# Compressed-branch scores as eight small tiles of the array, compressed values split in two, and chunk products in pairs, in a one-core transformer layer

## The chip, the core and the metric

The kernel runs on one core of a Trainium2 chip. The metric is the device time of one execution in microseconds (us). A core has a matrix engine (TensorE, PE in the profile, with its weight loads as PEld), a vector engine (VectorE, DVE), an activation engine (ScalarE, ACT), a general engine (GpSimd, POOL) and a queue that issues transfers (SyncE, SP). Each works through its own list of instructions in order and waits on semaphores for the others. PE reads SBUF and writes PSUM, which holds eight banks of 128 partitions by 512 float32 values here.

## What is computed

One decoder layer on 512 positions and 1024 features. One input projection feeds two token mixers; mixer A is sparse attention with a compressed, a selected and a window branch, mixer B a gated linear recurrence in chunks of 64. Both are gated, projected, summed, projected again and normalized.

```python
h = x @ w_in + b_in                          # 5912 columns, split into ten parts
kc, vc = compress(k_cmp, ...), compress(v_cmp, ...)       # 31 blocks per group
sc = einsum('bghqd,bgnd->bghqn', q, kc) * scale           # 8 heads, 2 groups
o_cmp = masked_softmax(sc, cmp_end <= t) @ vc
o_a = g0 * o_cmp + g1 * o_slc + g2 * o_win
attn = where(causal, einsum('bhncd,bhnsd->bhncs', qe, ke), 0)   # chunks of 64
o_b = attn @ v + carried state
y = sigmoid(gm_a) * (o_a @ w_branch_a) + sigmoid(gm_b) * (o_b @ w_branch_b)
x = layer_norm(alpha * x + y @ w_out)
```

With 512 positions the selected branch takes all eight blocks, so that both it and the window are plain causal attention.

## The kernel before

**Number formats.** Large products are made in three passes: each operand is split by `split2` (ACT copies it to float32r, DVE subtracts to get the rest), and hi·hi, hi·lo, lo·hi are summed in PSUM. A float32r product is one record in the trace. A product of plain float32 operands is two records.

**Stages.** The gate tiles of mixer B come first, then `proj(name)` makes one 128-column tile of the input projection after another in the order of `SEQ`: kcmp, vcmp, kslc, kwin, q0, q1, v, zb0, q2, zb1, q3, zb2, zb3, za0 to za3, then the sixteen gate tiles. A tile is 24 products of 512 columns. Then come the branch projections in the order of `BRANCH` (each entry two outputs of 12 products, written to a `pa` and a `pss` bank), and the output projection over four row blocks.

**What sets the order.** PE and SP keep the program's order. All smaller work is in generators ("chains") run by `_Weave`: every second step of a projection calls `tick()`, which lets each chain that is due go on to its next `yield`; the number yielded is the ticks to wait. The table `D` holds these numbers. ACT and DVE have their order fixed by the scheduler when the program is built.

**Mixer B.** `hgrn(h)` makes for each of four heads the chunk products `pst_`: four of 64 weight columns and 64 moving columns (first chunk of each pair with itself), four of 128 weight columns and 64 moving columns. `hgrn_norm` then sends the norms to all partitions with sixteen small SP transfers in a row and waits `n2` ticks.

**The compressed branch.** `cmp_kv` makes the compressed keys and values with three small float32 products in three `pst` tiles (two buffers); keys go to `kcB` in a block-diagonal form of 64 columns. `cmp_probs(c)`, for c = 0 and 1, multiplies each 128-row block of two query tiles `qraw` (weights) by `kcB` (64 moving columns): four products per query tile, 16 in all, in float32; the result has positions on partitions, so the softmax follows directly. It ends with `transpose4` into `PTc[c]`. `attn_values` begins with four float32 products of `vcB` and `PTc`, 512 columns each.

**Loads.** `load(i + 3)` puts the weights of a later tile into one of three `wraw` buffers, `split(i + 2)` splits them. Query tiles also issue four small SP transfers each (`rope`). The query tile's own copy out of PSUM is the ACT instruction at line 332 (in `evac`).

**The end.** In each branch step the kernel loads a block of the output weights (`load_out`), subtracts row means (`minus_mean`) and splits it. The output projection uses the banks `pa` and `pss` in turn, and at the last block also `pst`.

Of the kernel before, what the change touches and what calls it, by code (L numbers as in the profile page):

```python
# [43 lines left out]
BRANCH = [("b", 0), ("b", 2), ("a", 0), ("b", 4), ("a", 2), ("b", 6), ("a", 4), ("a", 6)]  # L44


def _columns(name):

    c = np.arange(_COLS[name], _COLS[name] + 128)
    if name[0] == "q" and name[1] != "b" or name[:2] == "za":  # L50
# [17 lines left out]
         r0=5, p0=5, p1=13, a0=1, a1=3, a2=1, a3=1, a4=1, a5=1, s0=14, s1=21, s2=0, s3=2)  # L68
# [27 lines left out]
def layer_kernel(ctx: ExitStack, tc: tile.TileContext, xT, xn, w0, wi, wf, wv, small, brow, consts,  # L96
# [141 lines left out]
    kcB = cst.tile([P, 64], F32, name="kcB")  # L238
# [4 lines left out]
    G.memset(kcB, 0.0)  # L243
# [121 lines left out]
    def hgrn(h):  # L365
# [44 lines left out]
        V.copy_predicated(at[0:64].rearrange("p (t s) -> p t s", s=128),  # L410
                          tri[0:64].unsqueeze(1).to_broadcast([64, 4, 128]),
                          pst_[0:64].rearrange("p (t s) -> p t s", s=128))
        V.copy_predicated(chunks(at[64:128])[:, :, 1],
                          tri[64:128, 64:128].unsqueeze(1).to_broadcast([64, 4, 64]),
                          chunks(pst_[64:128])[:, :, 1])
# [27 lines left out]
    def hgrn_norm():  # L443
# [19 lines left out]
        yield D["n2"]  # L463
# [31 lines left out]
    mvs, ready = [None, None], set()  # L495

    def cmp_kv():
# [24 lines left out]
        T.matmul(ps[:, 0:64], w2s[:, 0:128], hT[:, 0:64], start=True, stop=True)  # L522
        for g in range(2):
            V.tensor_copy(kcB[64 * g:64 * g + 64, 32 * g:32 * g + 32], ps[64 * g:64 * g + 64, 32 * g:32 * g + 32])
        for g in range(2):
            ps = PT()
            T.matmul(ps[:, 0:64], hT[:, 64 + 128 * g:192 + 128 * g], w2s[:, 128:192], start=True, stop=True)
            for m in range(4):
                r = 32 * (2 * (m % 2) + g)
                dst = vcB[r:r + 32, m, 64 * g:64 * g + 64]  # L530
                if m % 2:
                    V.tensor_copy(dst, ps[r:r + 32, 0:64])
                else:
                    A.copy(dst, ps[r:r + 32, 0:64])
        ready.add("cmp")

# [51 lines left out]
    def cmp_probs(c):  # L588
        while "cmp" not in ready:
            yield 1  # L590
        ps = PS()
        for m in range(2):
            for i in range(4):
                T.matmul(ps[:, 128 * i + 64 * m:128 * i + 64 * m + 64],
                         qraw[2 * c + m][:, 128 * i:128 * i + 128], kcB, start=True, stop=True)
            if m == 0:
                yield 1
        s = T2()
        s4 = s.rearrange("p (i h n) -> p i h n", i=4, n=32)
        s3 = s.rearrange("p (x n) -> p x n", n=32)  # L600
        mx = SM(16, "mx")
        V.tensor_tensor(s4, ps.rearrange("p (i h n) -> p i h n", i=4, n=32),
                        cmask.unsqueeze(2).to_broadcast([P, 4, 4, 32]), ALU.add)
# [14 lines left out]
        PTc[c] = T2()  # L618
        A.copy(PTc[c], ps)
# [47 lines left out]
    def attn_values():  # L667

        while len(PTc) < 2:
            yield 1  # L670
        for m in range(4):
# [110 lines left out]
    for name in SEQ:  # L782
# [8 lines left out]
        if name[0] == "q":  # L791
# [52 lines left out]

    y, rb = [], {}
    load_out(0)
    for n, (mix, m0) in enumerate(BRANCH):
# [3 lines left out]
        load_out(n + 1)  # L851
# [22 lines left out]
        hl = [(T2(dt=F32R), T2(dt=F32R)) for _ in range(2)]  # L874
        nm = minus_mean(woraw[n])
        for raw, (hi, lo) in zip(woraw[n], hl):
            A.activation(hi, raw, AF.Identity, bias=nm)
# [131 lines left out]
```

## Time and profile before

| | |
|---|---|
| time, median of 3 runs | 441.57 us (440.76 to 441.75) |
| the profiled execution | 441.97 us, of which the span is 440.2 us |
| PE busy | 431.6 us, 98% of the span |
| DVE busy, ACT busy, POOL busy | 299.4, 244.8 and 16.6 us |
| granted TensorE clock | 0.997 of full speed |
| chain that ended last | PE 89%, DVE 3%, SP queue 2%, ACT 2% |

The span runs from the first to the last instruction; about 1.8 us of the execution lie around it. A row of the timeline gives start, duration, engine, line, operation, output<-input tiles, shape and how many records (x) are merged. Matmuls overlap their successors, so that a product's price is the distance from its start to that of the next, and not its duration. "[0.77 <-ACT t L332]" says that the engine sat idle for 0.77 us and what ended the wait.

### The profile page before, as it was taken

What the parts mean: (1) busy time and instruction counts of PE and PEld (TensorE: products, weight loads), DVE (VectorE), ACT (ScalarE), POOL (GpSimd) and SP (SyncE); (2) the same over time, 40 slices, a digit from 0 to 9 for tenths busy, and PEclk for the clock granted to TensorE, in tenths of its full rate; (3) what the DMA queues carried; (4) which work ended last, traced back from release to release, by engine and by line L of the source; (5) the groups of instructions that cost most, each with busy time, mean ns of one, the idle gap of its engine ahead of it and who ended that gap; (6) DMA issues with size and microseconds to landing.
All of it is one profiled execution on the core that took longest, in us unless ns stands there. A gap on an engine that the chain in (4) does not pass through costs nothing.

```text
span 440.2 us, 6100 instructions
## 1 busy us (share of the span) xinstructions
PE 431.6 (98%) x2205; PEld 361.2 (82%) x2205; DVE 299.4 (68%) x619; ACT 244.8 (56%) x488; POOL 16.6 (4%) x28
## 2 busy tenths in 40 slices
PE   9999999999999999999999999999999999999994
PEld 8888888888898887887888888888888888878884
DVE  5815769986887339965664667666755598882675
ACT  4444625413447326679765676678955577657300
POOL 2000000000011310000000010001001100000000
PEclk9999999999999999999999999999999999999998
DMA  7996300342320363221211112111223452153121
GB/s 270 394 349 212 133 0 2 96 145 76 107 85 0 87 224 117 100 96 49 95 48 49 48 50 96 49 48 48 95 72 123 127 210 94 48 171 117 50 95 48
DMA packets 20878, 47.57 MB, mean 108 GB/s; under 512 B 2928, under 2 KB 4592, under 8 KB 20848
## 3 DMA queue, kind: packets, MB, share of 16 engines
q1 hardware_dynamic: 20560, 46.92, 31.4%
q8 instruction: 17, 0.28, 0.3%
q10 hardware_dynamic: 288, 0.26, 0.2%
q14 instruction: 13, 0.11, 0.1%
HBM read 41.93 MB, written 2.10 MB: 100 GB/s over the span
## 4 chain that ended last, share of the span: by engine, by line
PE 89%; DVE 3%; SPq 2%; ACT 2%; DMA 1%; issue 1%; POOL 0%; DVEq 0%; ACTq 0%
PE pa L104 56%; PE pss L104 19%; PE pso L104 10%; PE pst L108 4%; SPq L111 2%; DMA wraw<-in_wf_dram 1%; PE pst L104 1%; ACT whi L147 1%; DVE wlo L148 0%; ACT t L147 0%; DVE t L148 0%; DVE t L878 0%; DVE t L866 0%; POOL gat L317 0%; DVE t L926 0%
## 5 line engine op out<-in xcount | busy, mean ns | idle before, releaser
L104 PE MATMUL pa<-t,whi 128*128 128x512 f32 x640 | 203.4, 399 | 0.3 <-ACT t L811 0.3
L104 PEld LDWEIGHTS pa<-t,whi 128*128 128x128 f32 x640 | 116.8, 188 | 25.8 <-issue 2.3
L104 PE MATMUL pa<-t,wlo 128*128 128x512 f32 x320 | 125.2, 391 | 0.0
L148 DVE TENSOR_TENSOR wlo<-wraw,whi 128x1024 fp32r<-128x1024 f32 x46 | 56.7, 1234 | 29.8 <-ACT whi L147 29.8
L104 PEld LDWEIGHTS pa<-t,wlo 128*128 128x128 f32 x320 | 60.0, 188 | 13.2
L147 ACT CAST whi<-wraw 128x1024 fp32r<-128x1024 f32 x46 | 48.2, 1047 | 34.0 <-PE pa L104 16.0
L104 PE MATMUL pss<-t,t 128*128 128x512 f32 (+5 forms) x302 | 48.2, 315 | 0.0
L104 PE MATMUL pa<-t,t 128*128 128x512 f32 (+1 forms) x216 | 48.0, 379 | 0.1
L104 PEld LDWEIGHTS pa<-t,t 128*128 128x128 f32 x216 | 39.3, 188 | 7.9 <-DVE t L866 0.5
L104 PEld LDWEIGHTS pss<-t,t 128*128 128x128 f32 (+1 forms) x302 | 38.7, 173 | 6.5 <-issue 1.0
L651 ACT ACTIVATE t<-t,sm_mn 128x512 f32<-128x512 f32 (+3 forms) x64 | 35.8, 560 | 14.8 <-DVE sm_mn L648 13.7
L648 DVE CUSTOM_DVE_ANT_0 t<-pss,t 128x512 f32<-128x512 f32 (+3 forms) x64 | 30.1, 487 | 16.9 <-PE pss L104 16.8
L148 DVE TENSOR_TENSOR t<-pst,t 128x512 fp32r<-128x512 f32 x40 | 27.5, 689 | 15.8 <-ACT t L147 15.8
L147 ACT CAST t<-pst 128x512 fp32r<-128x512 f32 x40 | 23.1, 579 | 17.1 <-PE pst L108 16.9
L108 PE MATMUL pst<-con,t 128*128 128x128 f32 x181 | 27.4, 272 | 0.0
L108 PEld LDWEIGHTS pst<-con,t 128*128 128x128 f32 x181 | 22.4, 140 | 4.1
L104 PE MATMUL pso<-t,vv 128*128 128x512 f32 x80 | 23.1, 410 | 0.0
L104 PE MATMUL pso<-t,t 128*128 128x128 f32 (+2 forms) x110 | 21.8, 322 | 0.0
L148 DVE TENSOR_TENSOR t<-t,t 128x512 fp32r<-128x512 f32 (+1 forms) x22 | 14.2, 666 | 10.6 <-ACT t L147 10.5
L104 PE MATMUL pss<-t,whi 128*128 128x512 f32 x64 | 19.7, 389 | 0.0
L147 ACT CAST t<-t 128x512 fp32r<-128x512 f32 (+1 forms) x22 | 12.7, 603 | 12.5 <-DVE t L870 8.2
L662 ACT ACTIVATE t<-t,sm_dn 128x512 f32<-128x512 f32 (+3 forms) x32 | 16.6, 557 | 4.5 <-DVE sm_dn L657 4.5
(163 smaller groups left out, 522.7 us busy)
## 6 DMA issues: line engine op xcount, KB each, us to landing
wraw<-in_wf_dram SPq DMA_DIRECT2D x38, 512.0 KB, 3.5
wraw<-in_wbr_dram SPq DMA_DIRECT2D x8, 512.0 KB, 3.5
t<-in_wout_dram SPq DMA_DIRECT2D x16, 256.0 KB, 3.9
t<-in_w_dram SPq DMA_DIRECT2D x15, 256.0 KB, 5.4
t<-t SPq DMA_DIRECT2D x48, 64.0 KB, 2.0
t<-in_wi_dram SPq DMA_DIRECT2D x8, 256.0 KB, 6.0
t<-in_xn_dram SPq DMA_DIRECT2D x8, 256.0 KB, 6.2
out_dram<-t SPq DMA_DIRECT2D x8, 256.0 KB, 2.1
```

What stands on the lines that cost most here:

```text
L104: return tc.keep_in_program_order(nc.tensor.matmul(*a, **k))
L108: return tc.keep_in_program_order(nc.tensor.transpose(*a, **k))
L111: tc.keep_in_program_order(nc.sync.dma_start(o, i))
L147: A.copy(dst_hi, src)
L148: V.tensor_tensor(dst_lo, src, dst_hi.bitcast(F32), ALU.subtract)
L648: V.tensor_tensor_reduce(out=p[:, c], in0=ps[:, c], in1=amask[:, 512 - n:512], op0=ALU.add, op1=ALU.min, scale=-0.125, scalar=3.0e38, accu ...
L651: A.activation(p[:, c], p[:, c], AF.Exp, bias=mn[:, k], scale=-1.0, accum_out=den[:, k])
L662: A.mul(ts[m][:, c], ts[m][:, c], den[:, k])
```

## The change

1. **Scores features first.** `kcB` holds the keys of group g on partitions 64g to 64g + 63 and 32 columns. A new chain `cmp_scores` makes eight products, one for each query tile m and group g: weights `kcB` of 64 rows and 32 columns, the query tile moving with 512 columns, output on partitions 32m to 32m + 31 of one of two `pss` banks (one for each group). ACT and DVE copy one bank each, eight 128 by 128 transposes turn them in two groups of four, and four additions of the mask replace two. Two chains `cmp_probs(c, s)` follow with the softmax as it was.
2. **Values split.** `vcB` is split into `vcp`, and `PTc[c]` is written as hi and lo. Each of four float32 products becomes three float32r products.
3. **Chunk products in pairs.** In `hgrn` two products of 128 weight columns and 2 x 64 moving columns replace the four of 64 x 64; the blocks off the diagonal aren't read. The masked copies change to match (three in place of two).
4. **One bank in `cmp_kv`.** The three small products go into one `pst` tile.
5. **Order.** `hgrn_norm` yields 3 ticks after each four of its sixteen transfers. `BRANCH` has the third "b" entry before the first "a". `load_out` comes one step later, a block's split (`split_out`) two steps later, with two left after the last step. The output projection takes the banks `pst`, `pso`, `pa`, `pss` in turn. Several numbers of `D` change.

```diff
-BRANCH = [("b", 0), ("b", 2), ("a", 0), ("b", 4), ("a", 2), ("b", 6), ("a", 4), ("a", 6)]
+BRANCH = [("b", 0), ("b", 2), ("b", 4), ("a", 0), ("a", 2), ("b", 6), ("a", 4), ("a", 6)]
...
-         r0=5, p0=5, p1=13, a0=1, a1=3, a2=1, a3=1, a4=1, a5=1, s0=14, s1=21, s2=0, s3=2)
+         r0=5, p0=4, p1=11, p2=2, b0=1, a0=1, a1=1, a2=1, a3=1, a4=2, a5=1, s0=17, s2=0, s3=1)
...
-        for t in range(4):
-            T.matmul(pst_[0:64, 128 * t:128 * t + 64], ke[:, 64 * t:64 * t + 64],
-                     qeM[:, 128 * t:128 * t + 64], start=True, stop=True)
+        for u in range(2):
+            T.matmul(chunks(pst_)[:, 2 * u:2 * u + 2, 0], ke[:, 128 * u:128 * u + 128],
+                     qmc[:, 2 * u:2 * u + 2, 0], start=True, stop=True)
...
             for b in range(4):
                 dma(rms[h][32 * b:32 * b + 32], rs[32 * h:32 * h + 32])
-        yield D["n2"]
+            yield 3
+        yield D["n2"] - 9
...
-        T.matmul(ps[:, 0:64], w2s[:, 0:128], hT[:, 0:64], start=True, stop=True)
+        T.matmul(ps[:, 0:64], w2s[:, 0:128], hT[:, 0:64], start=True, stop=False)
         for g in range(2):
-            V.tensor_copy(kcB[64 * g:64 * g + 64, 32 * g:32 * g + 32], ps[64 * g:64 * g + 64, 32 * g:32 * g + 32])
+            T.matmul(ps[:, 64 + 64 * g:128 + 64 * g], hT[:, 64 + 128 * g:192 + 128 * g], w2s[:, 128:192],
+                     start=False, stop=g == 1)
...
+        vcp.extend((T2(dt=F32R), T2(dt=F32R)))
+        split2(vcB.rearrange("p m d -> p (m d)"), *vcp)
...
-    def cmp_probs(c):
+    def cmp_scores():
         while "cmp" not in ready:
             yield 1
-        ps = PS()
-        for m in range(2):
-            for i in range(4):
-                T.matmul(ps[:, 128 * i + 64 * m:128 * i + 64 * m + 64],
-                         qraw[2 * c + m][:, 128 * i:128 * i + 128], kcB, start=True, stop=True)
-            if m == 0:
-                yield 1
...
+        pg = PS(), PS()
+        for m in range(4):
+            for g in range(2):
+                gs = slice(64 * g, 64 * g + 64)
+                T.matmul(pg[g][32 * m:32 * m + 32], kcB[gs], qraw[m][gs], start=True, stop=True)
+        sT = T2(), T2()
+        A.copy(sT[0], pg[0])
+        V.tensor_copy(sT[1], pg[1])
+        yield D["p2"]
...
+        for g in range(2):
+            ps = transpose4(sT[g])
...
+            for c in range(2):
+                V.tensor_tensor(s6[c][:, g], p4[:, c], cmask.unsqueeze(2).to_broadcast([P, 4, 2, 32]), ALU.add)
+            yield 1
+        for c in range(2):
+            weave.start(cmp_probs(c, ss[c]), 2 * c)
...
-            T.matmul(po, vcB[:, m], PTc[m // 2], start=True, stop=True)
+            hi, lo = (t[:, 128 * m:128 * m + 128] for t in vcp)
+            T.matmul(po, hi, PTc[m // 2][0], start=True, stop=False)
+            T.matmul(po, hi, PTc[m // 2][1], start=False, stop=False)
+            T.matmul(po, lo, PTc[m // 2][0], start=False, stop=True)
...
-                weave.start(cmp_probs(0), D["s1"])
...
-                weave.start(cmp_probs(1), D["s3"])
+                weave.start(cmp_scores(), D["s3"])
...
-        load_out(n + 1)
+        load_out(n)
...
+        if n >= 2:
+            split_out(n - 2)
+    split_out(6)
+    split_out(7)
...
-        bank = (PA, PS)[tt % 2]
+        bank = (PT, PO, PA, PS)[tt]
```

PE, in the middle of tile zb2, before: the second half of the old scores. `pa` is the tile's bank, `whi` and `wlo` its split weights, `t_1564` and `t_1670` the query tiles q2 and q3.

```order
L104 MATMUL pss<-kcB,t_1564 128x64 x4
L104 MATMUL pa<-t_215,whi 128x512
L104 MATMUL pa<-t_216,whi 128x512
L104 MATMUL pa<-t_215,wlo 128x512
L104 MATMUL pa<-t_239,whi 128x512
L104 MATMUL pa<-t_240,whi 128x512
L104 MATMUL pa<-t_239,wlo 128x512
L104 MATMUL pss<-kcB,t_1670 128x64 x4
```

PE, in the same tile zb2, now: `t_1176` to `t_1646` are q0 to q3.

```order
L104 MATMUL pa<-t_142,wlo 128x512
L104 MATMUL pss<-t_1176,kcB 32x512 x2
L104 MATMUL pss<-t_1252,kcB 32x512 x2
L104 MATMUL pss<-t_1551,kcB 32x512 x2
L104 MATMUL pss<-t_1646,kcB 32x512 x2
L104 MATMUL pa<-t_166,whi 128x512
```

All eight stand together after the sixth product of zb2, where q3 was first read after the eighteenth; the groups of four transposes come after 12 and 18 further products.

SP's queue from tile zb0 to q3: `t_1478` (now `t_1475`) are the norms of mixer B, `wraw` the weights of tiles, `t_1551` the query tile q2.

```order
-L111 DMA t_1496<-t_1478 32x512 x4
-L111 DMA t_1501<-t_1478 32x512 x4
-L111 DMA t_1506<-t_1478 32x512 x4
-L111 DMA t_1511<-t_1478 32x512 x4
+L111 DMA t_1493<-t_1475 32x512 x4
+L111 DMA wraw<-in_wf_dram 128x1024
+L111 DMA t_1528<-t_1475 32x512 x4
+L111 DMA wraw<-in_wf_dram 128x1024
+L111 DMA t_1560<-t_1475 32x512 x4
+L111 DMA t_1565<-t_1551 32x512 x4
+L111 DMA t_1590<-t_1475 32x512 x4
```

The weights of zb2 and zb3, which stood behind all sixteen transfers, now stand behind four and eight; the transfers of q2 stand behind twelve of them and before the last four.

ACT from the end of tile q2 to that of q3, before: `whi<-wraw` splits weights, lines 809 and 811 read the bank of zb1, line 581 finishes q2's rotation, line 332 copies q2 and later q3 out of PSUM.

```order
L332 ACTIVATE t_1564<-pa,sml 128x512
L147 CAST whi<-wraw 128x1024 x2
L809 ACTIVATE t_1604<-pa,sml 128x512
L811 ACTIVATE t_1605<-pa,hbias 128x512
L581 CAST t_1630<-t_1574 64x512
L581 CAST t_1631<-t_1574 64x512
L147 CAST t_1653<-t_1148 128x512
L147 CAST whi<-wraw 128x1024
L332 ACTIVATE t_1670<-pa,sml 128x512
```

ACT over the same stretch now (lines 331, 828, 830 and 586 answer to 332, 809, 811 and 581).

```order
L331 ACTIVATE t_1551<-pa,sml 128x512
L147 CAST whi<-wraw 128x1024 x2
L828 ACTIVATE t_1601<-pa,sml 128x512
L830 ACTIVATE t_1602<-pa,hbias 128x512
L586 CAST t_1621<-t_1566 64x512
L586 CAST t_1622<-t_1566 64x512
L331 ACTIVATE t_1646<-pa,sml 128x512
```

The copy of q3 now stands right behind q2's two casts, with the next weights' cast after it.

## Rows read from the trace of the kernel before

**Rows 1.** The page's part on engines: busy us, share of the span, instructions.

```profile
PE 431.6 (98%) x2205; PEld 361.2 (82%) x2205; DVE 299.4 (68%) x619; ACT 244.8 (56%) x488; POOL 16.6 (4%) x28
```

**Rows 2.** Busy time by stretch: length, PE, PEld, DVE, ACT, POOL, clock, DMA.

```profile
200.00:300.00 100.00, 100.00 (x497) 82.69 (x496) 62.95 (x156) 70.56 (x154) 1.29 (x1) 1.00 0.17 58
```

**Rows 3.** Waits of PE: releaser, us in total, times, longest.

```profile
PE pss L104 <- ACT t L332: 0.8, 1, 0.8
PE pst L104 <- DVE kcB L524: 0.4, 1, 0.4
PE pa L104 <- ACT t L811: 0.3, 1, 0.3
```

**Rows 4.** Timeline of PE, chunk products of one head and the tile after them.

```profile
75.77 1.71 PE L104 MATMUL pss<-t,t 128*64 128x64 f32 x16
...
77.84 0.40 PE L104 MATMUL pa<-t,wlo 128*128 128x512 f32 x1
```

**Rows 5.** Chain that ended last: three float32 products, then twelve float32r.

```profile
90.54 0.67 PE pss L104 x6
...
351.81 2.72 PE pa L104 x12
```

**Rows 6.** Timeline of PE, old scores: first group and last group.

```profile
156.88 1.00 PE L104 MATMUL pss<-kcB,t 128*128 128x64 f32 x8
...
158.23 0.40 PE L104 MATMUL pa<-t,wlo 128*128 128x512 f32 x1
...
169.29 1.10 PE L104 MATMUL pss<-kcB,t 128*128 128x64 f32 x8 [0.77 <-ACT t L332]
```

**Rows 7.** Timeline of PE, norm sums of mixer B: four tiles of 32 columns.

```profile
137.20 0.93 PE L104 MATMUL pa<-t,t 128*128 128x280 f32 x6
138.06 1.07 PE L104 MATMUL pss<-t,ones 128*32 128x512 f32 x8
...
139.63 0.40 PE L104 MATMUL pa<-t,wlo 128*128 128x512 f32 x1
```

**Rows 8.** Timeline of PE, a group of four transposes.

```profile
214.23 0.60 PE L108 MATMUL pst<-con,t 128*128 128x128 f32 x4
...
215.14 0.39 PE L104 MATMUL pa<-t,wlo 128*128 128x512 f32 x1
```

**Rows 9.** Timeline of PE, one product of compressed values.

```profile
198.88 1.02 PE L104 MATMUL pso<-t,vcB 128*128 128x512 f32 x2
...
200.20 0.39 PE L104 MATMUL pa<-t,wlo 128*128 128x512 f32 x1
```

**Rows 10.** Timeline of SP's queue, the norms' transfers and the weights behind them.

```profile
142.96 10.97 SPq L111 DMA_DIRECT2D t<-t  x16
154.03 1.03 SPq L111 DMA_DIRECT2D wraw<-in_wf_dram  x2
```

**Rows 11.** DMA issues, 150 to 170 us: KB each, median us to landing.

```profile
t<-t SPq DMA_DIRECT2D x12, 64.0 KB, 2.0
```

**Rows 12.** Timeline of ACT: weights' casts, zb1, q2's casts, q3's copy; an output block's split.

```profile
157.58 1.05 ACT L147 CAST whi<-wraw 128x1024 fp32r<-128x1024 f32 x1 [6.62 <-DMA wraw<-in_wf_dram]
...
161.91 0.68 ACT L809 ACTIVATE t<-pa,sml 128x512 f32<-128x512 f32 x1
...
165.80 1.26 ACT L581 CAST t<-t 64x512 fp32r<-64x512 f32 x2 [2.63 <-DVE t L578]
...
168.56 0.68 ACT L332 ACTIVATE t<-pa,sml 128x512 f32<-128x512 f32 x1
...
394.56 1.33 ACT L877 ACTIVATE t<-t,sm_nm 128x512 fp32r<-128x512 f32 x2
```

**Rows 13.** Timeline of PE, the first two products of tile q3.

```profile
155.51 0.62 PE L104 MATMUL pa<-t,whi 128*128 128x512 f32 x2
```

**Rows 14.** Timeline of DVE, the last block's split of the output weights.

```profile
395.31 1.42 DVE L878 SCALAR_TENSOR_TENSOR t<-t,sm_nm,t 128x512 fp32r<-128x512 f32 x2
```

**Rows 15.** Chain that ended last: the output projection's first row block.

```profile
390.63 10.50 PE pa L104 x45
```

More of the change, by code (lines that the diff above doesn't have):

```diff
@@ L237, in layer_kernel @@
         G.memset(t, 0.0)
-    kcB = cst.tile([P, 64], F32, name="kcB")
+    kcB = cst.tile([P, 32], F32, name="kcB")
     vv = cst.tile([P, 4, 2, 256], F32R, name="vv")
@@ L242, in layer_kernel @@
     vcB = cst.tile([P, 4, 128], F32, name="vcB")
-    G.memset(kcB, 0.0)
     G.memset(vcB, 0.0)
@@ L409, in hgrn @@
         at = attn_sb[h]
[L410 to L415, printed above, removed]
+        for v in range(2):
+            V.copy_predicated(chunks(at[0:64])[:, v:4:2, 0],
+                              tri[0:64, 0:64].unsqueeze(1).to_broadcast([64, 2, 64]),
+                              chunks(pst_[64 * v:64 * v + 64])[:, v:4:2, 0])
+        V.copy_predicated(chunks(at)[:, :, 1], tri[:, 64:128].unsqueeze(1).to_broadcast([P, 4, 64]),
+                          chunks(pst_)[:, :, 1])
         yield D["h5"]
@@ L493, in cmp_hidden @@
         mvs[a] = mv
-    mvs, ready = [None, None], set()
+    mvs, ready, vcp = [None, None], set(), []
     def cmp_kv():
@@ L521, in cmp_kv @@
         ps = PT()
[L522 removed]
+        T.matmul(ps[:, 0:64], w2s[:, 0:128], hT[:, 0:64], start=True, stop=False)
         for g in range(2):
[L524 removed]
+            T.matmul(ps[:, 64 + 64 * g:128 + 64 * g], hT[:, 64 + 128 * g:192 + 128 * g], w2s[:, 128:192],
+                     start=False, stop=g == 1)
         for g in range(2):
[L526 to L527 removed]
+            V.tensor_copy(kcB[64 * g:64 * g + 64], ps[64 * g:64 * g + 64, 32 * g:32 * g + 32])
+        for g in range(2):
             for m in range(4):
                 r = 32 * (2 * (m % 2) + g)
[L530 removed]
+                dst, src = vcB[r:r + 32, m, 64 * g:64 * g + 64], ps[r:r + 32, 64 + 64 * g:128 + 64 * g]
                 if m % 2:
[L532 removed]
+                    V.tensor_copy(dst, src)
                 else:
[L534 removed]
+                    A.copy(dst, src)
         ready.add("cmp")
+        yield 2
+        vcp.extend((T2(dt=F32R), T2(dt=F32R)))
+        split2(vcB.rearrange("p m d -> p (m d)"), *vcp)
     gat = cst.tile([P, 4, 24], F32, name="gat")
@@ L617, in cmp_probs @@
         ps = transpose4(s)
-        PTc[c] = T2()
-        A.copy(PTc[c], ps)
+        PTc[c] = T2(dt=F32R), T2(dt=F32R)
+        split2(ps, *PTc[c])
     units = [(i, brs) for i in range(3, -1, -1) for brs in (((0,), (1,)) if i >= 2 else ((0, 1),))]
@@ L843, in minus_mean, with split_out @@
         return nm
+    def split_out(kt):
+        hl = [(T2(dt=F32R), T2(dt=F32R)) for _ in range(2)]
+        nm = minus_mean(woraw[kt])
+        for raw, (hi, lo) in zip(woraw[kt], hl):
+            A.activation(hi, raw, AF.Identity, bias=nm)
+            V.scalar_tensor_tensor(lo, raw, nm, hi.bitcast(F32), ALU.add, ALU.subtract)
+        wo.append(hl)
     y, rb = [], {}
-    load_out(0)
     for n, (mix, m0) in enumerate(BRANCH):
@@ L873, in layer_kernel @@
                 y.append(hl)
[L874 to L877, printed above, removed]
-            V.scalar_tensor_tensor(lo, raw, nm, hi.bitcast(F32), ALU.add, ALU.subtract)
-        wo.append(hl)
+        if n >= 2:
+            split_out(n - 2)
+    split_out(6)
+    split_out(7)
     for hf in range(2):
```

10 lines of the change are left out of this document (6 added, 4 removed).

## The prediction

> **What bounds the kernel now.** I read the engines' shares first, then a stretch, then PE's waits. PE is busy 431.6 us of a span of 440.2, DVE 68% and ACT 56% of it [rows 1]. From 200 to 300 us PE is busy for 100.00 of 100 us at full clock, DVE for 63 and ACT for 71 [rows 2]. PE's waits inside the program are short, the longest 0.8 us [rows 3]. So the kernel is bound by PE, a product taken out of its list is worth its whole distance to the next start, and what DVE and ACT gain or lose counts only where PE waits for it.
>
> The working is by PE's list. A group is priced from its own start to the start of the later product with the low weights in the tile's next row, less two plain products, so that the extra time at the change of number format or of weight shape is in it. A plain float32r product of 512 columns costs 2.72 / 12 = 0.227 us, and a float32 product of 128 columns 0.67 / 3 = 0.223 [rows 5].
>
> **Chunk products, four heads.** Before, the eight products of a head cost 77.84 - 75.77 - 0.454 = 1.62 us [rows 4]. Now there are four of 128 weight columns and 64 moving ones, which is the shape of a group of the old scores, 158.23 - 156.88 - 0.454 = 0.90 [rows 6], and two of 128 by 128, 2 x 0.223 = 0.45. That is 1.35, a saving of 0.27 per head and 1.1 in all. If the two wide ones cost no more than 64 columns do it is somewhat more, and if much of 1.62 is a gap that stays it is less: 0.7 to 1.5. The masked copies grow by one DVE instruction per head; DVE idles a third of the time.
>
> **One bank in cmp_kv.** The third product waited 0.4 us for a copy out of one of only two buffers [rows 3]. One bank takes that wait away: 0.4.
>
> **Scores.** Before: four groups at 0.90, 3.6 us [rows 6]. Now: a burst of eight products of 64 rows, 32 weight columns and 512 moving columns, and two groups of four transposes. No product of the trace uses half the rows. The nearest row is the norm sums of mixer B: four products of 32 weight columns and 512 columns, each on its own quarter of the array, eight records. The six records ahead of it began at 137.20 and take 6 x 0.129 = 0.77 by their columns, which puts the burst's turn at 137.97; up to 139.63 less 0.454 that is 1.2 us for all four [rows 7]. One float32 product of 512 columns alone costs 200.20 - 198.88 - 0.454 = 0.87 [rows 9], and four of these 3.5, so the quarters clearly work at once. I take it that both halves of the rows also work at once, since products on different rows and different columns share neither weights nor outputs: 1.2 for eight. If the halves take turns it is one more pass, 0.85, and if all eight go one after the other it is 8 x 0.86 = 6.9. A group of transposes costs 215.14 - 214.23 - 0.454 = 0.46 [rows 8], two 0.92. The saving is 3.6 - 1.2 - 0.92 = 1.5; with halves in turn 0.65; in a row, a loss of 4.2.
>
> The row of the norm sums bears on this: a group in another shape of the array does not cost its neighbours more than the 0.1 us or so that lie in the 1.2 [rows 7]. The Trainium skill (page "TensorEngine Tiling (Array Packing)", section "Key Properties") says that a change of tiling mode drains TensorE, which speaks against a burst between full-size products, and that different tiles load weights and multiply in parallel, which speaks for it. The trace shows the drain as small, and of row tiles it shows nothing; by the second rule the burst would be the 1.2 above, and the total is unchanged.
>
> **Values.** Four float32 products cost 0.87 each, 3.46 [rows 9]. Twelve float32r ones cost 12 x 0.227 = 2.73. The saving is 0.7. The splits add two instructions for `vcB` and one more for each `PTc`, each under 0.7 us and long before the attention that reads them begins.
>
> **The two waits at q3.** PE waits 0.8 us for the copy of q3 at line 332 and 0.3 for zb1's bank at line 811 [rows 3]. Their cause is SP. Its sixteen norm transfers take 10.97 us, 0.69 each, and only then, at 154.03, come the next weights [rows 10]. ACT has nothing else ahead in its list and idles 6.62 us for them; so its read of zb1 begins at 161.91, q2's casts at 165.80 and q3's copy at 168.56 [rows 12]. Now the weights of zb2 stand behind four transfers and those of zb3 behind eight, 12 x 0.69 = 8.3 and 8 x 0.69 = 5.5 us sooner. What is late next? PE began q3 at 155.51 [rows 13]; less 1.1 and 0.4 that is 154.0, when zb1's bank is complete. zb3's cast needs a free buffer then, 1.05 us, and zb1 can be read from about 155.4 instead of 161.91. q2's rotation goes out behind twelve transfers and two weights, 142.96 + 12 x 0.69 + 1.0 = 152.3 to 154.7, and has landed 2.0 later [rows 10, 11], at 156.7. With DVE's two or three steps in between at about 0.7 (half of the pair in [rows 14]) q2's casts begin between 158.2 and 160 and take 1.3, and q3's copy of 0.7 follows them. PE has q3 done at 154.0 + 24 x 0.227 = 159.5 and stands at the scores six products later, at 160.8. The copy is done between 160.5 and 161.8, and only the last two of the eight products read q3, which gives them up to 0.9 more. A wait of 0 to 0.8 is left; I take 0.3, so of 1.1 us of waits 0.8 goes.
>
> **Edits put at nothing.** DVE gets some five more instructions and ACT three, covered by the idle third of DVE. The output weights' splits now stand two steps later, with two blocks after the last step: two on ACT of 1.33 [rows 12] and two on DVE of 1.42 [rows 14]. The last of them ended at 395.31 + 1.42 = 396.7 before; with 2.8 more it is 399.5. The last block's first product is the 43rd of the output projection, 390.63 + 42 x 0.227 = 400.2 [rows 15]. That leaves 0.7; beyond it PE would wait for the overrun. Four banks in turn for four row blocks need no bank twice, and the tail after PE stays. The other order of `BRANCH` keeps the number of products.
>
> **Sum.** 1.1 + 0.4 + 1.5 + 0.7 + 0.8 = 4.5 us. The profiled execution took 441.97, so this makes 437.5 of it; it lies 0.4 above the median of 441.57, and against the median the forecast is **437.1**. With the bounds (chunks 0.7 to 1.5, waits 0.3 to 1.1, burst 0.9 to 1.6, splits at the end 0 to 0.8 late) its own range is 435.3 to 438.5.
>
> **Rivals.**
>
> *Row halves take turns, or q3 is somewhat late.* The burst costs 0.85 more, or PE waits one to three us for q3's copy, with a saving of 4.5 less 0.9 to 3.4. For it: no row shows half-row products, and q3's copy stands behind q2's two casts, which wait for a rotation through SP. Against it: the quarters do work at once [rows 7]. It gives 438 to 440.5. Chance 0.16.
>
> *New waits in the attention or at the end.* The order of scores and transposes within an attention unit shifts with the new `D`, and the splits at the end have only 0.7 us of room. For it: ACT is at 71% in the stretch [rows 2]. Against: PE lost nothing there. It gives 438 to 441. Chance 0.05.
>
> *Slower: q3's copy as late as now.* All eight products stand at the place where PE arrives at 160.8, and in PE's list nothing else goes ahead of them. Before, q3 was read twelve products and a group later. If q2's rotation still ends when it did, the copy ends at 168.56 + 0.68 = 169.2 [rows 12], and the seventh product waits from about 161.3: 7.9 us, in place of the 0.3 of the sum. 437.1 + 7.9 - 0.3 makes about 444.7. It decides for slower as soon as the wait passes 4.8 us, that is with a copy ending after 166. For it: the copy stands right behind the casts of q2, and those stood behind DVE steps [rows 12]. Against: these DVE steps stood behind weights that came late, and the weights are 5.5 to 8.3 us sooner. Chance 0.08.
>
> *The eight products run one after the other* (the tiles don't do what the change says): 5.7 us more than in the sum, 442.8. The four quarters of [rows 7] speak against it. Chance 0.03.
>
> **How the numbers follow.** The forecast's chance is 0.68. Slower by over 0.2% (0.9 us, about what a measurement of this kernel can tell from no change) is the third and fourth rival with part of their neighbourhood, 0.09 after leaving out what of them ends near no change. Within 0.2%, from 440.7 to 442.5, are the far end of the first two and part of the fourth, 0.07. Faster is the rest, 0.84. The range goes from the low end of the forecast's own, 435.3, to 440.0, which takes in most of the first two rivals, and leaves out the slower ones and the ends.
>
> **What would show it.** PE's busy time should fall to about 428, with the waits for lines 332 and 811 and for `kcB` gone or below 0.5. The timeline should show the chunk products of a head at about 1.35 us up to the next product, and the burst as sixteen records in about 1.2; 2.05 would mean halves in turn, 6.9 none at once. On ACT, the idle time before the weights' casts near 157 us should be nearly gone and q3's copy stand at 160 to 161. The stretch from 200 to 300 should still be full, and the output projection without a gap. The prediction is wrong if PE waits for q3's copy by more than a microsecond, if the burst is longer than 2 us, or if a new wait stands in PE's list in the attention or at the last block.

## The result, and the profile after

The changed kernel takes 437.70 us (median; 437.17 to 438.06) against 441.57 before: a ratio of 0.9914, with an interval of 0.990 to 0.9928. It is faster by 3.9 us. The forecast was 437.1, with a range of 435.3 to 440.0. The profiled execution took 437.94 us with a span of 436.1, 4.1 less than the span of before.

The page of the changed kernel, the part on engines:

```profile
PE 428.6 (98%) x2185; PEld 359.6 (82%) x2185; DVE 304.3 (70%) x629; ACT 245.2 (56%) x490; POOL 16.3 (4%) x27
```

PE's busy time fell from 431.6 [rows 1] to 428.6, and the forecast was about 428. PE's waits in the changed kernel (releaser, us in total, times, longest):

```profile
PE pso L104 <- DVE t L159: 1.1, 1, 1.1
PE pst L104 <- DVE t L869: 0.3, 1, 0.3
```

The first line stands at the start of the program, and the kernel before has it too. All three waits of [rows 3] are gone from this list. A new one stands in their place: a product of the output projection (bank `pst`) waits for line 869, the split of an output block. The list counts only time in which PE is idle by its records; a shorter wait, such as the one for q3's copy inside the burst (below), shows only in the distances of starts.

The timeline of PE, changed kernel: the start of the program, chunk products of one head with the tile behind them, the burst of scores with the tile behind it, one product of compressed values, and the output projection's first row block:

```profile
4.06 2.66 PE L104 MATMUL pso<-t,t 128*128 128x256 f32 x12
...
76.36 1.45 PE L104 MATMUL pss<-t,t 128*128 128x128 f32 x12
...
78.16 0.39 PE L104 MATMUL pa<-t,wlo 128*128 128x512 f32 x1
...
161.11 1.45 PE L104 MATMUL pss<-t,kcB 64*32 64x512 f32 x16
...
163.06 0.40 PE L104 MATMUL pa<-t,wlo 128*128 128x512 f32 x1
...
198.99 0.84 PE L104 MATMUL pso<-t,t 128*128 128x512 f32 x3
199.67 0.62 PE L104 MATMUL pa<-t,whi 128*128 128x512 f32 x2
...
385.20 7.37 PE L104 MATMUL pst<-t,t 128*128 128x512 f32 x31
392.85 4.20 PE L104 MATMUL pst<-t,t 128*128 128x512 f32 x17 [0.28 <-DVE t L869]
```

With the prediction's own way of pricing (start to the row of the low weights, less 0.454) the chunk products cost 78.16 - 76.36 - 0.454 = 1.35 us, the burst 163.06 - 161.11 - 0.454 = 1.50, and a product of values 199.67 - 198.99 = 0.68.

The starts of the 24 products of each tile, which both kernels make in the same order, tell where the time went. I set the start of each tile after against that of the same tile before:

| place | change of the offset, us | what lies there | forecast |
|---|---|---|---|
| first 26 us | +0.67 | the same instructions, slower in this execution | 0 |
| 70 to 105 us | -1.46 | chunk products, four heads | -1.1 |
| 130 to 139 us | -0.52 | `cmp_kv` | -0.4 |
| 156 to 177 us | -2.73 | scores, burst, transposes, the two waits | -1.5 - 0.8 |
| 177 to 385 us | -0.51 | values (-0.75), small new gaps (+0.24) | -0.7 |
| 385 us to the end of PE | +0.45 | wait for line 869 (+0.67), a gap of before (-0.22) | 0 |

The sum is -4.1, the difference of the two spans. Without the first and the last row it would be -5.2. The one profile of before flatters the fourth row: against a second profile of the same kernel (before_again, below) it is -1.78 in place of -2.73, and the time from the first tile on falls by 3.79 us, close to the 3.9 of the medians.

The queue of SP, changed kernel, from the first norms to the weights behind q2's rotation:

```profile
142.69 2.40 SPq L111 DMA_DIRECT2D t<-t  x4
145.19 0.53 SPq L111 DMA_DIRECT2D wraw<-in_wf_dram  x1
145.76 2.41 SPq L111 DMA_DIRECT2D t<-t  x4
148.27 0.53 SPq L111 DMA_DIRECT2D wraw<-in_wf_dram  x1
148.90 8.24 SPq L111 DMA_DIRECT2D t<-t  x12
157.24 1.02 SPq L111 DMA_DIRECT2D wraw<-in_wf_dram  x2
```

ACT over that stretch, changed kernel (idle time before an instruction and what ended it in brackets):

```profile
154.19 1.06 ACT L147 CAST whi<-wraw 128x1024 fp32r<-128x1024 f32 x1 [3.59 <-PE pa L104]
155.15 0.68 ACT L828 ACTIVATE t<-pa,sml 128x512 f32<-128x512 f32 x1
...
159.48 1.26 ACT L586 CAST t<-t 64x512 fp32r<-64x512 f32 x2 [3.07 <-DVE t L583]
160.77 0.69 ACT L331 ACTIVATE t<-pa,sml 128x512 f32<-128x512 f32 x1
```

The weights no longer release ACT: in place of the 6.62 us for a transfer [rows 12] it waits 3.59 us for PE. zb1 is read at 155.15 (forecast 155.4), and q3's copy ends at 161.46 (forecast between 160.5 and 161.8).

### The profile page after: what moved, and what is told of

Its sections match the earlier page's. It is cut to its first block, busy times and chain, and to the rows that moved or that the text cites. A ratio compares the mean times of both kernels' runs of the same rounds, so it can differ in the third digit from the quotient of the medians.

```text
span 436.1 us, 6086 instructions
## 1 busy us (share of the span) xinstructions
PE 428.6 (98%) x2185; PEld 359.6 (82%) x2185; DVE 304.3 (70%) x629; ACT 245.2 (56%) x490; POOL 16.3 (4%) x27
## 4 chain that ended last, share of the span: by engine, by line
PE 93%; DVE 5%; ACT 1%; issue 0%; DVEq 0%; ACTq 0%
PE pa L104 59%; PE pss L104 15%; PE pso L104 12%; PE pst L108 5%; PE pst L104 2%; DVE t L869 1%; DVE t L892 1%; DVE t L148 1%; ACT t L147 1%; DVE t L896 1%; DVE wlo L148 0%; DVE t L950 0%; DVEq L1029 0%; DVE sm_nm L861 0%; DVE sm_bst L938 0%
## 5 line engine op out<-in xcount | busy, mean ns | idle before, releaser
L148 DVE TENSOR_TENSOR t<-pst,t 128x512 fp32r<-128x512 f32 x42 | 28.9, 690 | 17.3 <-ACT t L147 17.2
L104 PE MATMUL pso<-t,t 128*128 128x512 f32 (+2 forms) x170 | 36.9, 352 | 0.0
L104 PE MATMUL pa<-t,t 128*128 128x512 f32 (+1 forms) x168 | 36.7, 375 | 0.0
L104 PE MATMUL pss<-t,t 128*128 128x512 f32 (+4 forms) x238 | 36.1, 307 | 0.0
L147 ACT CAST t<-pst 128x512 fp32r<-128x512 f32 x42 | 24.3, 579 | 20.4 <-PE pst L108 20.3
L104 PEld LDWEIGHTS pa<-t,t 128*128 128x128 f32 x168 | 30.3, 188 | 5.6
L104 PEld LDWEIGHTS pss<-t,t 128*128 128x128 f32 (+1 forms) x238 | 29.3, 176 | 3.7 <-DMA wraw<-in_wf_dram 0.4
L104 PEld LDWEIGHTS pso<-t,t 128*128 128x128 f32 x170 | 28.2, 196 | 4.2
L108 PE MATMUL pst<-con,t 128*128 128x128 f32 x189 | 28.6, 272 | 0.0
```

The source lines that it names most:

```text
L104: return tc.keep_in_program_order(nc.tensor.matmul(*a, **k))
L108: return tc.keep_in_program_order(nc.tensor.transpose(*a, **k))
L147: A.copy(dst_hi, src)
L148: V.tensor_tensor(dst_lo, src, dst_hi.bitcast(F32), ALU.subtract)
```

## The experiments

The last column gives the time from the start of the first tile of the projection to the start of PE's last product in the profiled execution. It leaves out the first 26 us, where executions of the same PE instructions differ. Each ratio is to runs of the kernel before made beside it, whose medians lie between 441.13 and 441.57, so that ratios compare better than medians.

| kernel | median, us | ratio to before, interval | first tile starts at | from there to PE's last start |
|---|---|---|---|---|
| before | 441.57 | 1 | 26.39 | 407.41 |
| before_again | 440.88 | 0.9992 (0.9983 to 1.0002) | 26.69 | 406.45 |
| changed | 437.70 | 0.9914 (0.990 to 0.9928) | 27.06 | 402.66 |
| e1_pairs_back | 439.09 | 0.9951 (0.9934 to 0.9969) | 26.63 | 405.29 |
| e2_full_rows | 438.90 | 0.9940 (0.9918 to 0.9962) | 26.46 | 403.38 |
| e3_splits_before | 438.27 | 0.9929 (0.9918 to 0.9941) | 26.49 | 403.14 |
| e4_norms_in_row | 443.16 | 1.0043 (1.0027 to 1.0059) | 26.42 | 406.69 |
| e5_before_spread | 441.24 | 0.9997 (0.9987 to 1.0006) | 27.27 | 405.79 |
| e6_split_ahead | 437.63 | 0.9925 (0.9909 to 0.9941) | 26.27 | 403.87 |
| e7_scores_later | 438.20 | 0.9926 (0.9913 to 0.9938) | 27.46 | 402.60 |
| e8_both | 437.94 | 0.9923 (0.9911 to 0.9935) | 26.79 | 402.59 |
| e9_norms_on_dve | 437.70 | 0.9918 (0.9904 to 0.9931) | 26.66 | 402.87 |
| e10_splits_5_6 | 437.46 | 0.9910 (0.9896 to 0.9923) | 26.46 | 402.71 |
| e11_both | 437.85 | 0.9916 (0.9903 to 0.9930) | 26.54 | 402.87 |

### Do eight small products run at once? (e2, e7)

**e2_full_rows**: the same eight products on all rows, one group after the other.

```diff
-        for m in range(4):
-            for g in range(2):
-                gs = slice(64 * g, 64 * g + 64)
-                T.matmul(pg[g][32 * m:32 * m + 32], kcB[gs], qraw[m][gs], start=True, stop=True)
+        for g in range(2):
+            for m in range(4):
+                T.matmul(pg[g][32 * m:32 * m + 32], kcB[:, 32 * g:32 * g + 32], qraw[m], start=True, stop=True)
```

(and `kcB` of 64 columns, with zeros in the other group's rows, as in the kernel before.)

> The changed kernel with the eight score products on all 128 rows (zeros in the other group's rows of the weights), 32 columns as now, one group after the other, so that four can run at once but not eight. Theory: eight half-row products run at once in one turn, so that two turns cost 0.85 us more, less what the wait for q3's copy (0.36) hides: time 0.5 to 0.85 higher, 438.2 to 438.5. Rival: the row halves already take turns, and nothing changes, 437.7.

**e7_scores_later**: the burst one tick further on.

```diff
-         ... s0=17, s2=0, s3=1)
+         ... s0=17, s2=0, s3=2)
```

> The changed kernel with the scores' burst one tick later (s3=2 in place of 1), three products of zb2 further on. Theory: the 0.36 us between the sixth and the seventh product in the burst is the wait for q3's copy, which ended at 161.46; a tick later it is gone, the burst costs about 1.14 instead of 1.50 and the time is 0.3 lower, about 437.4. Rival: the 0.36 is the price of the second half of the burst itself (the array does not take all eight at once), and stays; time 437.7.

PE's timeline at the burst, first of e2_full_rows:

```profile
160.49 2.18 PE L104 MATMUL pss<-t,kcB 128*32 128x512 f32 x16
...
163.16 0.40 PE L104 MATMUL pa<-t,wlo 128*128 128x512 f32 x1
```

and of e7_scores_later:

```profile
162.87 1.09 PE L104 MATMUL pss<-t,kcB 64*32 64x512 f32 x16
...
164.46 0.40 PE L104 MATMUL pa<-t,wlo 128*128 128x512 f32 x1
```

In e7, where q3's copy is done before PE arrives, the eight cost 164.46 - 162.87 - 0.454 = 1.14 us; on full rows they cost 2.22. Not all of the 2.22 is the second turn, since q3's copy is late there too. ACT in e2_full_rows, and PE up to 160.70:

```profile
160.01 0.69 ACT L332 ACTIVATE t<-pa,sml 128x512 f32<-128x512 f32 x1
160.49 0.63 PE L104 MATMUL pss<-t,kcB 128*32 128x512 f32 x3
```

Three products have begun by 160.70; the fourth, which reads q3, begins at 160.76, right after the copy, and its column tile stays 0.27 behind to the end. Two turns alone thus cost about 1.95 (an estimate: 2.22 less 0.27), where the prediction had 2.05, and the row tiles alone save about 0.8. So halves of the rows do work at once, and the rival that they take turns has fallen. From the first tile on, e2 is 0.72 longer than the changed kernel, which is 2.22 less 1.50, as expected; its median rose by 1.2, more than expected, though the intervals of the two ratios overlap. The 1.50 of the changed kernel is 1.14 and a wait of 0.36 for q3's copy, as e7's theory had it: its copy ends at 161.46, and the seventh product begins at 161.51.

Yet e7's median, 438.20, is no lower than the changed kernel's, and from the first tile on it is 0.06 shorter in the trace rather than 0.36. With the chain a tick later, gaps in the attention grew: of 0.29 us at 305.9 and 0.19 at 308.7, where the changed kernel has one of 0.20 at 304.5 (each as a start distance over the usual one). What PE gained at 163 us it lost again behind it: 0.28 of the 0.36 by these gaps.

### What is the order on SP worth? (e4, e5, before_again)

**e4_norms_in_row**, from the changed kernel:

```diff
                 dma(rms[h][32 * b:32 * b + 32], rs[32 * h:32 * h + 32])
-            yield 3
-        yield D["n2"] - 9
+        yield D["n2"] + 3
```

> The changed kernel with the sixteen norm transfers in a row again, PE's order unchanged, so that SP has the weights of zb2 and zb3 and q2's rotation behind all of them. Theory: zb1's bank is read late again, zb2 starts about 3.5 us later than now (163.2 instead of 159.7), q3's copy ends near 167.8 and the burst's seventh product waits for it; about 6 us more than the changed kernel, 443.5, slower than the kernel before. Rival: the transfers' place matters no more than the 1.1 us of waits that the trace of before shows, 438.8.

**e5_before_spread**, from the kernel before, the opposite edit and nothing else:

```diff
                 dma(rms[h][32 * b:32 * b + 32], rs[32 * h:32 * h + 32])
-        yield D["n2"]
+            yield 3
+        yield D["n2"] - 9
```

> The kernel before with nothing changed but the norm transfers, four at a time with three ticks between. Theory: the waits for q3's copy and for zb1's bank go, 1.1 us by the rows of waits and 1.3 by the distances of starts: 440.3. Rival: the old scores need the wait anyway (q3's copy is set by its own products), 441.5.

**before_again**: the kernel before, unchanged.

> The kernel before once more, for a second profile of it: whether the waits ahead of q3's scores (1.36 us by the distances of starts) and the first 26 us of its one profile are typical. Theory: both vary from one execution to the next, the start by up to 1 us and the wait with what POOL and DVE do to each other, and the profiled execution had more of the wait than most; time 441.1 to 441.5. Rival: the wait is the same to 0.2 us.

PE's timeline around the burst of e4_norms_in_row:

```profile
160.30 0.73 PE L104 MATMUL pa<-t,whi 128*128 128x512 f32 x2 [1.13 <-ACT t L829]
...
161.90 1.07 PE L104 MATMUL pss<-t,kcB 64*32 64x512 f32 x12
164.90 1.05 PE L104 MATMUL pss<-t,kcB 64*32 64x512 f32 x4 [1.93 <-ACT t L331]
```

With the transfers in a row the changed kernel is slower than the kernel before, 443.16 us, 5.5 over itself; 6 was expected. In the profile PE waits for zb1's bank and then, in the middle of the burst, for q3's copy, and the time from the first tile on is 4.0 us longer than in the changed kernel. This profile is of the fastest of the ten executions, 441.27 us. The others reach 444.49, and the five above 443 us have a mean granted clock of 0.989 to 0.994, where no execution of another kernel here is below 0.995. In these five the clock thus stood longer at the lower of its two levels, 1.2 GHz. Their traces are not at hand, and how the rest of the 5.5 divides between waits and clock stays open. This is the mechanism of the prediction's slower rival, at about 5.5 us of the 7.6 that it gave: the burst can stand where it does only because the norm transfers make way.

The same edit made alone in the kernel before gains nothing that the times show (0.9997). Its two waits are gone from the trace, and from the first tile on its profiled execution is 1.62 us shorter than that of before; but the second profile of the kernel before is itself 0.96 shorter than the first, with a wait of only 0.4 us there:

```profile
PE pss L104 <- ACT t L332: 0.4, 1, 0.4
```

where [rows 3] has 0.8 and another 0.3. ACT's second weight cast of that stretch, first in the profile of before, then in that of before_again:

```profile
160.96 1.05 ACT L147 CAST whi<-wraw 128x1024 fp32r<-128x1024 f32 x1 [2.33 <-DMA wraw<-in_wf_dram]
160.31 1.05 ACT L147 CAST whi<-wraw 128x1024 fp32r<-128x1024 f32 x1 [1.13 <-DMA wraw<-in_wf_dram]
```

Counted from the first tile the second is 0.95 us sooner (133.62 for 134.57), which is the whole difference of the two profiles, while the steps of DVE and POOL take the same time in both. The wait of before thus varies with how soon the weights land, and not with what DVE and POOL do to each other, as had been expected; and the one profile on which the prediction rested had more of it than the second. How much of it the median of before contains is open: e5's interval allows up to 0.6 us and no more.

### Chunk products (e1)

**e1_pairs_back**:

```diff
-        for u in range(2):
-            T.matmul(chunks(pst_)[:, 2 * u:2 * u + 2, 0], ke[:, 128 * u:128 * u + 128],
-                     qmc[:, 2 * u:2 * u + 2, 0], start=True, stop=True)
+        for t in range(4):
+            T.matmul(pst_[0:64, 128 * t:128 * t + 64], ke[:, 64 * t:64 * t + 64],
+                     qeM[:, 128 * t:128 * t + 64], start=True, stop=True)
```

(and the two masked copies of before.)

> The changed kernel with the chunk products of 64 by 64 as before. Theory: 0.36 us per head come back, 0.27 within the group and 0.09 at the change of shape ahead of its first product, 1.45 in all: 439.1. Rival: only the 0.27 of the prediction, 438.8; or the masked copies, which are one fewer on DVE again, give something back.

The median rose by 1.39, as expected, and the tiles behind the four heads start 1.47 later against the first tile. But the trace, of the slowest of the six executions (440.09), holds more than that: 2.63 us from the first tile on. The rest is at the burst. PE's timeline of e1_pairs_back:

```profile
162.11 1.07 PE L104 MATMUL pss<-t,kcB 64*32 64x512 f32 x12
163.71 1.05 PE L104 MATMUL pss<-t,kcB 64*32 64x512 f32 x4 [0.52 <-ACT t L331]
```

q3's copy came late, although PE itself arrived a microsecond later than in the changed kernel. Its cause is a DVE step of q2's rotation, line 583. DVE in e1_pairs_back:

```profile
159.87 1.78 DVE L583 TENSOR_TENSOR t<-t,t 128x512 f32<-128x512 f32 x1
```

and POOL there:

```profile
159.62 1.48 POOL L469 TENSOR_TENSOR t<-t,t 128x512 f32<-128x512 f32 x1 [2.62 <-DMA t<-t]
```

DVE in the changed kernel:

```profile
158.77 0.68 DVE L583 TENSOR_TENSOR t<-t,t 128x512 f32<-128x512 f32 x1
```

and POOL there:

```profile
158.83 1.77 POOL L469 TENSOR_TENSOR t<-t,t 128x512 f32<-128x512 f32 x1 [2.93 <-DMA t<-t]
```

Where POOL's product by the last norm begins 0.25 us ahead of line 583, DVE takes 1.78 us for it instead of 0.68. Where DVE begins 0.06 ahead, it takes 0.68, and POOL 1.77 instead of the 1.29 of its product at 154.60. The two seem to hold each other up, and whichever begins first goes through: a lead of 0.06 us was enough for DVE.

### Do DVE and POOL hold each other up? (e9)

**e9_norms_on_dve**:

```diff
-            G.tensor_tensor(o, o, rms[h], ALU.mult)
+            V.tensor_tensor(o, o, rms[h], ALU.mult)
```

> The changed kernel with the four products by the norms (line 469) on DVE in place of POOL. Theory: DVE and POOL hold each other up: the DVE step at line 583 takes 0.68 us alone but 1.78 where a POOL product began just before it, and q2's casts, q3's copy and the burst follow it. With POOL out, line 583 and the casts' partners take their plain durations, q3's copy ends about 0.5 to 0.8 earlier against zb2's start than in the changed kernel, and the burst's 0.36 wait goes: 0.3 to 0.6 less than the changed kernel's median (437.1 to 437.4), with less spread between runs. Rival: the long DVE steps come from something else (transfers into SBUF), stay long, and the four more steps on DVE make q3's copy later: 438 or more.

DVE in e9_norms_on_dve:

```profile
154.83 1.22 DVE L148 TENSOR_TENSOR wlo<-wraw,whi 128x1024 fp32r<-128x1024 f32 x1 [2.21 <-ACT whi L147]
155.97 0.68 DVE L469 TENSOR_TENSOR t<-t,t 128x512 f32<-128x512 f32 x1
...
158.44 0.69 DVE L583 TENSOR_TENSOR t<-t,t 128x512 f32<-128x512 f32 x1
```

With no product on POOL the long steps are gone: 1.22 us for a weight split that takes 1.70 in the changed kernel, and 0.69 for line 583. The transfers, the rival, are still there. So the mutual hold is shown. The time is not better, 437.70, nor is the spread smaller (437.34 to 438.46): the product that DVE now makes itself at 155.97 takes 0.60 to the next start, where the split gave back 0.48. q3's copy ends at 161.13, 0.47 after PE begins the burst (0.35 in the changed kernel), and the burst costs 1.63 (1.50 there). The mechanism held, and the gain expected from it did not come.

### The wait at the end (e3, e6, e8, e10, e11)

DVE in the changed kernel, at the end of the branch steps:

```profile
389.24 0.68 DVE L892 SCALAR_TENSOR_TENSOR t<-t,pss 128x512 f32<-128x512 f32 x1
...
391.42 0.69 DVE L148 TENSOR_TENSOR t<-t,t 128x512 fp32r<-128x512 f32 x1 [0.74 <-ACT t L147]
392.05 4.07 DVE L869 SCALAR_TENSOR_TENSOR t<-t,sm_nm,t 128x512 fp32r<-128x512 f32 x6
```

Six splits, of blocks 5, 6 and 7, stand behind the last output. PE needs the first low part of block 5 with its 32nd product, and the start before it is 385.20 + 30 x 0.227 = 392.0; it is ready at 392.05 + 0.69. That is the gap before 392.85: 0.56 us over the usual distance, and 0.11 more at the next start.

**e3_splits_before**: loads and splits as in the kernel before.

```diff
-        load_out(n)
+        load_out(n + 1)
...
-        if n >= 2:
-            split_out(n - 2)
-    split_out(6)
-    split_out(7)
+        split_out(n)
```

(and `load_out(0)` ahead of the loop.)

> The changed kernel with the loads and splits of the output weights as they were before (a block loaded one step ahead, split in its own step). Theory: the gap of 0.79 us between two starts in the first row block of the output projection, at 392.07 us, comes from the split of block 5 standing on DVE behind the last branch outputs; with the old timing it goes, and the time falls by about 0.6 us, to 437.1. Rival: the gap is one of the branch outputs themselves, and stays at 437.7.

The gap at the end went, and another came, in PE's waits of e3_splits_before:

```profile
PE pa L104 <- DVE t L893: 0.7, 1, 0.7
```

In the last branch step PE now waits for DVE to empty a bank. The wait had moved from one place to another.

**e6_split_ahead**: the split of block n - 2 ahead of the step's products. **e10_splits_5_6**: that, and block 6 between the last two outputs.

```diff
         load_out(n)
+        if n >= 2:
+            split_out(n - 2)
...
-        if n >= 2:
-            split_out(n - 2)
```

```diff
                 y.append(hl)
+            if n == 7 and m == m0:
+                split_out(6)
...
-    split_out(6)
     split_out(7)
```

> The changed kernel with each block's split ahead of its step's branch products, so that block 5 is split before the last branch outputs, and blocks 6 and 7 after them as now. Theory: block 5's low part is ready several us early; block 6's first half would be ready at about 392.8 for its use at 393.4, block 7's at about 394.2 for 394.9, so no wait is left and the time falls by 0.6 to about 437.1. Rival: the wait only moves to block 6 or 7, with less than 0.3 gained.

> The changed kernel with each block's split ahead of its step's outputs, and block 6's between the two outputs of the last step, so that only block 7 is split after them. Theory: the 0.56 us wait, which moved from block 5 to block 6 when only block 5 was put ahead, has no third place to go to: block 7's first low part is ready about 0.7 after the last output's split and needed 1.4 later. The first row block is without a gap, 0.6 less, 437.1. Rival: the outputs behind the splits come later by as much, and the gap stays.

PE's timeline of e10_splits_5_6:

```profile
384.70 10.10 PE L104 MATMUL pst<-t,t 128*128 128x512 f32 x43
395.07 1.43 PE L104 MATMUL pst<-t,t 128*128 128x512 f32 x5 [0.28 <-DVE t L869]
```

The gap is now before the 44th product, block 7's low part; in e6 it was at block 6 (before 394.66). Its size stayed 0.28 by the list of waits each time. DVE in e10_splits_5_6 shows why:

```profile
391.50 0.68 DVE L894 SCALAR_TENSOR_TENSOR t<-t,pss 128x512 f32<-128x512 f32 x1
...
393.64 0.69 DVE L148 TENSOR_TENSOR t<-t,t 128x512 fp32r<-128x512 f32 x1 [0.74 <-ACT t L147]
394.27 1.41 DVE L869 SCALAR_TENSOR_TENSOR t<-t,sm_nm,t 128x512 fp32r<-128x512 f32 x2
```

PE ended the last branch output at about 384.7, and DVE comes to reading it at 391.50. It carries a backlog of nearly seven us out of the branch steps, and each output costs it a turn to ACT and back (0.74 idle). A split put ahead delays the outputs behind it: the last one is read at 391.50 here and at 389.24 in the changed kernel, 2.3 us later with two pairs of splits of 1.42 put ahead. Both rivals held. 437.46 is the lowest median of all, but within the interval of the changed kernel.

**e8_both** is e6 and e7 together, **e11_both** e9 and e10.

> Split ahead and scores a tick later together. Theory: the two waits are independent, since PE is never idle between them, and the gains add to about 1.0: 436.7. Rival: what PE gains at 161 is lost again in a wait further on, 437.1.

> Norm products on DVE and blocks 5 and 6 split ahead, together. Theory: both waits go, about 1.0 us less than the changed kernel: 436.7. Rival: one gives back what the other brings, 437.3.

Neither gain appeared: 437.94 and 437.85. No version beat the changed kernel by more than can be measured.

## Why the prediction was right, and where its steps were off

**The bound.** Right: PE's list sets the time. From 200 to 300 us the changed kernel shows (columns as in [rows 2])

```profile
200.00:300.00 100.00, 100.00 (x503) 83.68 (x502) 65.21 (x163) 71.88 (x162) 1.28 (x1) 1.00 0.18 58
```

and 3.9 us of the 4.5 forecast arrived. The bounds that the sum lists do not give its own range: with 437.1 in the middle they make 436.1 to 439.2, and not 435.3 to 438.5. The measured 437.70 lies in both.

**Chunk products.** The group costs 1.35 as worked out, but the saving is 0.36 per head and not 0.27 (1.46 in all; e1 gave 1.47). The missed 0.09 lies ahead of the group's first product: I priced from the group's own start, and the change of shape ahead of the 64-column products, which goes too, stands before that start.

**cmp_kv and values.** 0.52 and 0.75 for 0.4 and 0.7. The list of waits says 0.4 where the start distance says 0.52, since a wait also costs the overlap of the next product.

**Scores.** Right, by the choice of the norm sums as the nearest row: 1.14 alone against 1.2 forecast. e2 shows the first rival's price, about 1.95 for two turns of four. That the wait for q3 came out at 0.36 against 0.3 is partly luck. In e6_split_ahead, whose instructions there are the same, the burst costs 2.68, a wait of 1.54, because a POOL product began ahead of line 583:

```profile
157.82 1.45 POOL L469 TENSOR_TENSOR t<-t,t 128x512 f32<-128x512 f32 x1 [2.64 <-DMA t<-t]
158.05 1.78 DVE L583 TENSOR_TENSOR t<-t,t 128x512 f32<-128x512 f32 x1
```

The prediction had no such hold in its sum; by its own signs it counts as wrong when PE waits for q3 by more than a microsecond. The Trainium skill ("TensorEngine Tiling (Array Packing)", "Key Properties") has different tiles loading and multiplying in parallel, and the trace agrees (1.14 for eight in one turn, about 1.95 in two). The same section of the Trainium skill has a change of tiling mode drain TensorE; the bursts show no more than about 0.1 us over the usual distance at either end.

**The waits at q3.** Right in mechanism (ACT released by PE in place of the weights; zb1 within 0.3 us of the forecast, q2's casts and q3's copy inside the stretches given for them), and e4 shows that without the new order on SP the rival would have decided, at 443.2 for the 444.7 forecast (its profile shows a part of that as waits, as said above). Off in size for the median: taken from one execution that had more of the wait than the next one (0.4 in before_again for 0.8 and 0.3). e5 leaves at most 0.6 for it.

**Edits put at nothing.** This is the step that failed. I checked the last block against PE's need and found 0.7 us of room. But the splits come out of DVE in the order 5, 6, 7 behind the last output, and block 5 is needed 12 products, 2.7 us, sooner than block 7. It costs 0.67 us by start distances, near the far end of the "0 to 0.8 late" of the range, where the sum took nothing; a gap there was also one of the signs of being wrong. The room of 0.7 was itself miscounted. The row of 45 records in [rows 15] begins with the fourth product of the projection, as PE's timeline of before shows with all 48:

```profile
389.73 11.40 PE L104 MATMUL pa<-t,t 128*128 128x512 f32 x48
```

So the 43rd starts at about 399.6 and not 400.2, and the room against 399.5 was next to nothing. The rival of a new wait at the end did occur, and the larger gains elsewhere covered it.

**The profiled execution** also lost 0.67 us in its first 7 us, with PE instructions that are the same in both kernels; that is no part of the change, and the last section has its cause.

## What to carry to other kernels

Small products on disjoint rows and columns of the array can run at once (here eight for 1.14 us, where one of full size costs 0.87), so a burst pays; but it gathers all its operands' waits in one place, and whatever stands ahead of the last operand (here sixteen small transfers on SP) must be cleared first: the same edit on SP was worth 5.5 us by the medians with the burst and nothing that shows without it. When splits or copies are put behind the last outputs, check the first block that is used and not the last, and look at how far behind the engine already is: moving work within a backlog moves the wait and does not shorten it. A wait read from one execution is one sample; a second profile of the same kernel is cheap and more than halved this one.

## What was not expected of the hardware

**DVE and POOL block each other.** A DVE product of two SBUF operands took 1.78 us instead of 0.68 when a POOL product had begun 0.25 us earlier, and POOL 1.77 instead of 1.29 when DVE had begun 0.06 earlier. The Trainium skill ("SBUF — State Buffer", "Who interferes with whom") says that a DVE instruction with two inputs in SBUF contends with a GpSimd instruction that reads SBUF, and that the order of issue decides which of them blocks. The trace agrees with both, down to the order of starts. In this kernel it moves q3's copy by 1.1 us: line 583 took 1.78 us in e6_split_ahead too (its rows stand above), and its burst cost 1.18 us more.

**The first 26 us vary.** The start of the first tile lay anywhere between 26.27 and 27.46 us in the fourteen profiles, with the same PE instructions ahead of it. In the kernel before the row that answers to the changed kernel's 2.66 us is

```profile
4.06 1.99 PE L104 MATMUL pso<-t,t 128*128 128x256 f32 x12
```

In both, the 14 records ahead of it come about 0.21 us apart. In the kernel before, those of 256 columns come 0.12 apart from 4.69 us on, and in the changed kernel at 0.21 until 6.07 and at 0.12 from there. 256 columns in 0.21 us are 1.2 columns per ns, which fits the lower of the clock's two levels, 1.2 GHz, though the column of the granted clock shows 1.00 for both. That column counts time without a record as full clock. In the traces the record of full clock begins at 4.35 us in the kernel before and at 5.98 in the changed one, just ahead of the faster spacing; PE had made nothing but these first products until then. In the fourteen profiles it begins between 3.93 and 6.92 us, and the three latest (5.98, 6.06 and 6.92, in changed, e5 and e7) belong to the three latest first tiles (27.06, 27.27 and 27.46). What decides the moment was not tested. A difference of less than a microsecond between two single profiles of this program says nothing until this part is taken off.
